# Attention probabilities kept as float32 and multiplied with the values as float32 products, two heads side by side

## The chip, the cores and the metric

The kernel runs on one core of one Trainium2 chip. The metric is the device time of one execution in microseconds (us), the median of several runs; less is better. Besides, one execution was recorded by the hardware profiler. Its engines are named as in the profile: PE is TensorE's matmul, PEld its weight load, DVE VectorE, ACT ScalarE, POOL GpSimd, SP SyncE, which issues the DMAs.

## The reference

A two-layer encoder on 1024 tokens of width 1024 in float32. The first layer mixes tokens by grouped-query attention, the second by a pooling mixer; each layer then cross-attends into 256 memory tokens and applies a gated MLP. The change touches the attention of the first layer alone, 16 query heads of width 64 that share 4 key and value heads:

```python
def axial_gqa_attention(h, w_qkv, q_gain, k_gain, w_o):
    ...
    def attend_block(q_blk):
        scores = jnp.einsum('bkgqd,bksd->bkgqs', q_blk, kt).astype(jnp.float32)
        p = jax.nn.softmax(scores, axis=-1).astype(vt.dtype)
        return jnp.einsum('bkgqs,bksd->bkgqd', p, vt)

    o = lax.map(attend_block, qb)
    o = o.transpose(1, 0, 4, 2, 3, 5).reshape(b, s, N_HEADS * HEAD_DIM)
    return o @ w_o
```

The softmax is over all 1024 keys (no mask).

## The kernel before

Nearly all products are done in a reduced float32 type (`float32r`, fp32r in the profile). To keep precision an operand is split in two such numbers, a high part (a cast) and a low part (what the cast left out), and the products of the parts are added. One tile pool of 20 slots of 128 x 2048 (`R`) holds the operands; `scr` is a ring of six 128 x 1024 float32 buffers.

The queries, keys and values come from a stage whose order a planner works out (engines, due times, a greedy schedule). It ends with the scores and softmax of the first three units (0 to 2). The values lie in two slots `V`, for each key block of 128 and each of the 4 value heads 128 columns: 64 of the high part, 64 of the low part.

Then comes the loop of the attention, whose order is written out by hand: each engine runs its instructions in the order of the program. A unit is 128 queries of one head; `units` lists (j, hh, i): j of 4 pairs of query blocks, hh of 16 heads, i of the two blocks of a pair: 128 units, numbered u. PSUM holds two score buffers of two banks each (`pA`) and four single banks (`pB`). The parts:

- `scores(u)`, L789: four products of 512 columns into one `pA`.
- `peak(u)`, L1189, on DVE: the negated row maximum. `softmax(u)`: exp with its sum on ACT (L1195), the sum's inverse on POOL as a power (L1197), the scaling on POOL (L1198). The probabilities are in a `scr` buffer, queries on the partitions.
- `turned(u)`, L1209: eight 128 x 128 transposes into two banks; ACT casts each bank into the high part (L1211). `lows(u)`, L1216: DVE subtracts that from the bank for the low part. `PT` holds two sets of a high and a low tile, one set for the two units of a head.
- `values(u)`, for odd u: both units of the head, so 256 columns. For each of 8 key blocks two products (L1231 with the high, L1232 with the low probabilities), with the 128 columns of values, high and low, loaded: the bank's upper and lower half have to be summed in the end. ACT copies one half into `osum` (L1237).
- `add(u)`: DVE adds the other half (L1243); at each second head POOL splits the sum of two heads into high and low part (L1246, L1247) in the slots `OT`, the operand of the output projection.

A turn of the loop treats two units: scores(u), peak(u), turned and lows of u-3 and u-2, softmax(u), scores(u+1), then `values(u - 3)`, peak(u+1), `add(u - 3)`, softmax(u+1). The last turns are written out one by one, with the values of the last heads between the transposes. After the loop the output projection follows (L756 to L758), and the rest of the kernel.

Of the kernel before, what the change touches and what calls it, by code (L numbers as in the profile page):

```python
# [23 lines left out]
HD = 64  # L24
NH = 16
NKV = 4
# [604 lines left out]
class Kernel:  # L631
# [140 lines left out]
    def attention(self):  # L772
        nc, R, a, tc = self.nc, self.R, self.a, self.tc
# [3 lines left out]
        V = [R.get() for _ in range(2)]  # L777
        units = [(j, hh, i) for j in range(NT // 2) for hh in range(NH) for i in range(2)]
        Q, prs, OT, sums = {}, {}, [], {}

        def score(u):
            j, hh, i = units[u]
            kv = hh // 4
            c0 = (j % 2 + 2 * i) * P
            q = R.v(Q[kv, j // 2], 4)[:, hh % 4, c0:c0 + P]
            s = self.psA()
            for kh in range(2):
                for part in range(2):
                    nc.tensor.matmul(s[:, kh * 512:(kh + 1) * 512], q,  # L789
                                     R.v(K[part][kh], 4)[:, kv],  # L790
                                     start=part == 0, stop=part == 1)
            return s

        with tc.tile_pool(name="qk", bufs=1, reuse_waits="tile") as qk, self.psum("psq", 1, 6) as self.ps:
# [3 lines left out]
            tabs, at, where = {"Q": tab}, {}, {}  # L798
# [22 lines left out]
            g = {"Q": self.cst.tile([P, HD], F32, name="gq"), "K": self.cst.tile([P, HD], F32, name="gk")}  # L821
# [351 lines left out]

        self.ps = self.ctx.enter_context(self.psum("ps", 2, 4))
        with tc.tile_pool(name="at", bufs=1, reuse_waits="tile") as at:
            PT = [[at.tile([P, 2048], F32R, name=f"PT{i}{j}") for j in range(2)] for i in range(2)]
            def parts(u):
                return (x.rearrange("p (a b) -> p a b", a=8) for x in PT[u // 2 % 2])

            S, nm, T = {}, {}, {}  # L1180

            def scores(u):
                if u not in prs:
                    S[u] = score(u)

            def peak(u):
                if u in S:
                    nm[u] = self.stat(1, "nm")
                    nc.vector.tensor_reduce(nm[u], S[u], axis=AX.X, op=OP.max, negate=True)  # L1189

            def softmax(u):
                if u in S:
                    pr = prs[u] = self.scr()
                    rs = self.stat(1, "sum")
                    nc.scalar.activation(pr, S.pop(u), AF.Exp, bias=nm.pop(u), accum_out=rs)  # L1195
                    ri = self.stat(1, "inv")
                    nc.gpsimd.tensor_tensor(out=ri, in0=rs, in1=self.minus, op=OP.pow)  # L1197
                    nc.gpsimd.tensor_scalar(pr, pr, ri, 1.0, op0=OP.mult, op1=OP.mult)  # L1198

            def pieces(u, g):  # L1200
                c = slice(u % 2 * P, (u % 2 + 1) * P)
                return (x[:, 4 * g:4 * g + 4, c] for x in parts(u))

            def turn(u, g):
                if u in prs:
                    p = T[u, g] = self.psB().rearrange("p (a b) -> p a b", a=4)
                    for k in range(4):
                        b = 4 * g + k
                        nc.tensor.transpose(p[:, k, :], prs[u][:, b * P:(b + 1) * P], self.ident)  # L1209
                    hi, _ = pieces(u, g)  # L1210
                    nc.scalar.copy(hi, p)  # L1211

            def low(u, g):
                if (u, g) in T:
                    hi, lo = pieces(u, g)
                    nc.vector.tensor_tensor(out=lo, in0=T.pop((u, g)), in1=hi.bitcast(F32), op=OP.subtract)  # L1216
                    if g:
                        del prs[u]

            def values(u, blocks=range(NT)):  # L1220
                if u > 0:
                    j, hh, i = units[u]
                    if blocks[0] == 0:
                        O[u] = self.psB()[:, :256]
                        if hh == 0:
                            OT.append([R.get(), R.get()])
                    ph, pl = parts(u)
                    o = O[u]
                    for kt in blocks:
                        v = R.tiles[V[kt // 4]].rearrange("p (k h c) -> p k h c", k=4, h=4)[:, kt % 4, hh // 4, :]  # L1230
                        nc.tensor.matmul(o, v, ph[:, kt], start=kt == 0, stop=False)  # L1231
                        nc.tensor.matmul(o, v, pl[:, kt], start=False, stop=kt == NT - 1)  # L1232
                    if blocks[-1] < NT - 1:
                        return
                    if hh % 2 == 0:
                        sums[0] = at.tile([P, 256], F32, name="osum", bufs=2)
                    nc.scalar.copy(sums[0][(hh % 2) * HD:(hh % 2 + 1) * HD], o[HD:])  # L1237

            def add(u):
                if u in O:  # L1240
                    j, hh, i = units[u]
                    oo = sums[0][(hh % 2) * HD:(hh % 2 + 1) * HD]
                    nc.vector.tensor_tensor(out=oo, in0=O.pop(u)[:HD], in1=oo, op=OP.add)  # L1243
                    if hh % 2:
                        hi, lo = (R.v(x, 8)[:, hh // 2] for x in OT[j])
                        nc.gpsimd.tensor_scalar(hi, sums[0], 1.0, 1.0, op0=OP.mult, op1=OP.mult)  # L1246
                        nc.gpsimd.tensor_tensor(out=lo, in0=sums[0], in1=hi.bitcast(F32), op=OP.subtract)  # L1247
                    if hh % 4 == 3 and j % 2:
                        R.put(Q[hh // 4, j // 2])

            O = {}
            with tc.manual_schedule():
                def turned(u):
                    for g in range(2):
                        turn(u, g)

                def lows(u):
                    for g in range(2):
                        low(u, g)

                def shared(u):

                    scores(u)
                    peak(u)
                    turned(u - 3)
                    turned(u - 2)
                    lows(u - 3)
                    lows(u - 2)
                    softmax(u)
                    scores(u + 1)  # L1270

                last = len(units) - 1
                for u in range(0, last - 1, 2):
                    shared(u)
                    values(u - 3)
                    peak(u + 1)
                    add(u - 3)
                    softmax(u + 1)
                shared(last - 1)
                peak(last)  # L1280
                turned(last - 2)
                lows(last - 2)
                softmax(last)
                values(last - 4)
                add(last - 4)
                turned(last - 1)
                lows(last - 1)
                values(last - 2, range(NT // 2))
                turned(last)
                lows(last)  # L1290
                values(last - 2, range(NT // 2, NT))
                add(last - 2)
                values(last)
                add(last)
            R.put(*V, *K[0], *K[1])
        return OT

# [8 lines left out]
    def cross(self, i, X, steps=None, mixer=None, over={}):  # L1306
# [168 lines left out]
        def plan_turn(plan, t):  # L1475
# [8 lines left out]
            def part(g, j):  # L1484
                if t % 2 not in PT:
                    PT[t % 2] = [R.get_pair() for _ in range(4)]
                pairs = PT[t % 2][2 * g:2 * g + 2]
                src = sm["ps", t][g].rearrange("p (a b) -> p a b", a=4)
                same = all(one[0] == other[0] for one, other in pairs[:j + 1])
                for ks in [slice(0, 4)] if same else [slice(0, 2), slice(2, 4)]:  # L1490
                    hi, lo = (R.blocks(z, ks, slice(t // 2 * P, (t // 2 + 1) * P)) for z in pairs)
                    self.low(hi, lo, src[:, ks]) if j else self.high(hi, src[:, ks])
            plan.add("turn", 8, emit, both(t), sorted(set(banks)), [("A", banks[0])] if t % 2 else [("B", k) for k in banks])
            for g in range(2):
                k = ("PT", t, g)
                plan.add("copy", 512, partial(part, g, 0), [banks[g]], [k], (), banks[g:g + 1], room=(("PT", t % 2), 8))
# [779 lines left out]
```

## Time and profile before

| | |
|---|---|
| median of 2 runs | 2498.97 us (2498.05 to 2499.89) |
| span of the profiled execution | 2493.0 us |
| the attention loop in it | about 178 to 528 us |
| matmuls of the loop's values (L1231, L1232) | 2 x 512, in 64 groups of 16 |
| scores (L789), transposes (L1209) | 512, 1024 |

The page gives busy time by engine, the chain of work that ended last and the groups of instructions; the trace can be asked for windows of time, for groups in a window and for the order of instructions (timeline). In a timeline a row is: start in us, duration in us, engine, line, operation, output and inputs, partitions x elements; a row with x4 merges four like instructions. In a group the count is followed by the total busy time in us and the mean duration in ns, then by the idle time before and what ended it. For a matmul, 128*128 128x512 stands for the loaded operand (rows*columns) and the one streamed through.

### The profile page before, as it was taken

The numbers are of one execution on the slowest core, as the hardware profiler recorded it, in microseconds if no ns is written. First come the engines' busy times: TensorE is split into PE (matmuls) and PEld (weight loads), VectorE is DVE, ScalarE is ACT, GpSimd is POOL, SyncE is SP. The second block draws the span as 40 slices with busy tenths as digits, with TensorE's granted clock in tenths as the row PEclk, the third lists the DMA queues.
The fourth block names the chain that finished last, engine by engine and source line by source line (L and its number), as shares of the span: only waits on it lengthen the run. The fifth ranks groups of instructions, "written<-read, shape, count | busy, mean of one in ns | idle before, by whom it ended". The sixth has DMA issues, their size and how long they took to land.

```text
span 2493.0 us, 37178 instructions
## 1 busy us (share of the span) xinstructions
PE 2474.6 (99%) x13510; PEld 2138.3 (86%) x13510; DVE 1991.6 (80%) x2839; ACT 1351.0 (54%) x2326; POOL 462.1 (19%) x658
## 2 busy tenths in 40 slices
PE   9999999999999999999999999999999999999998
PEld 9999999988899888888888888889888888888887
DVE  7879999974986389888889676997469888888875
ACT  6558888862655255455555334655345545554542
POOL 5767777731011000000000003102010000000001
PEclk9999999999999999999999999999999999999999
DMA  5300000042585124343258553388123324337852
GB/s 170 100 4 1 2 1 1 2 165 69 202 311 181 62 70 127 89 123 106 85 178 290 196 176 112 128 299 300 65 72 114 110 85 127 106 93 257 276 193 98
DMA packets 310124, 320.73 MB, mean 129 GB/s; under 512 B 13229, under 2 KB 244765, under 8 KB 309941
## 3 DMA queue, kind: packets, MB, share of 16 engines
q1 hardware_dynamic: 309941, 318.35, 38.8%
q8 instruction: 107, 1.75, 0.3%
q14 instruction: 76, 0.62, 0.1%
HBM read 230.91 MB, written 82.58 MB: 126 GB/s over the span
## 4 chain that ended last, share of the span: by engine, by line
PE 93%; issue 2%; DVE 2%; POOL 1%; ACT 1%; DMA 1%; SPq 0%; POOLq 0%; ACTq 0%; DVEq 0%
PE pB L756 22%; PE pB L758 22%; PE pB L757 22%; PE pA L789 5%; PE pB L1209 4%; PE pA L758 3%; PE pA L756 3%; PE pA L757 3%; PE pB L1231 2%; PE pB L1232 2%; PE pB L325 1%; DVE R L672 1%; PE pB L1072 1%; PE pA L2164 0%; DMA scr<-X 0%
## 5 line engine op out<-in xcount | busy, mean ns | idle before, releaser
L756 PE MATMUL pB<-R,R 128*128 128x512 f32 (+1 forms) x2732 | 1014.8, 371 | 1.8 <-ACT R L669 0.9
L758 PE MATMUL pB<-R,R 128*128 128x512 f32 (+1 forms) x2728 | 1007.6, 369 | 1.7 <-DVE R L672 1.6
L757 PE MATMUL pB<-R,R 128*128 128x512 f32 (+1 forms) x2732 | 1008.8, 369 | 0.2 <-DVE R L672 0.2
L756 PEld LDWEIGHTS pB<-R,R 128*128 128x128 f32 x2732 | 514.7, 188 | 90.9 <-ACT R L669 2.1
L758 PEld LDWEIGHTS pB<-R,R 128*128 128x128 f32 x2728 | 513.9, 188 | 89.5 <-DVE R L672 3.5
L757 PEld LDWEIGHTS pB<-R,R 128*128 128x128 f32 x2732 | 514.9, 188 | 87.1 <-DVE R L672 1.2
L669 ACT ACTIVATE R<-scr 128x512 fp32r<-128x512 f32 (+2 forms) x340 | 256.8, 782 | 214.9 <-DMA scr<-Gs 59.8
L729 POOL TENSOR_SCALAR ms<-ss 128x1 f32<-128x1 f32 (+2 forms) x97 | 32.1, 331 | 1651.7 <-ACT R L737 1279.9
L672 DVE TENSOR_TENSOR R<-X,R 128x512 fp32r<-128x512 f32 x374 | 252.0, 685 | 67.8 <-ACT R L669 67.1
L669 ACT ACTIVATE R<-X 128x512 fp32r<-128x512 f32 x374 | 231.8, 630 | 132.9 <-PE pB L757 64.0
L672 DVE TENSOR_TENSOR R<-scr,R 128x512 fp32r<-128x512 f32 (+2 forms) x328 | 275.0, 867 | 26.6 <-ACT R L669 26.2
L439 ACT COPY scr<-pB 128x512 f32<-128x512 f32 x156 | 91.3, 585 | 180.6 <-PE pB L758 173.3
L1852 DVE TENSOR_TENSOR X<-pB,X 128x512 f32<-128x512 f32 (+1 forms) x145 | 99.2, 685 | 80.4 <-PE pB L758 79.6
L1216 DVE TENSOR_TENSOR PT<-pB,PT 128x512 fp32r<-128x512 f32 x256 | 159.1, 683 | 4.2 <-ACT PT L1211 2.9
L1189 DVE TENSOR_REDUCE nm<-pA 128x1 f32<-128x1024 f32 x125 | 152.2, 1218 | 4.3
L756 PE MATMUL pA<-R,R 128*128 128x512 f32 (+1 forms) x420 | 150.6, 359 | 0.0
L758 PE MATMUL pA<-R,R 128*128 128x512 f32 (+1 forms) x420 | 150.2, 358 | 0.0
L757 PE MATMUL pA<-R,R 128*128 128x512 f32 (+1 forms) x420 | 149.9, 357 | 0.0
L1195 ACT ACTIVATE scr<-pA,nm 128x1024 f32<-128x1024 f32 x125 | 142.4, 1139 | 5.6 <-DVE nm L1189 3.5
L789 PE MATMUL pA<-R,R 128*128 128x512 f32 x512 | 144.7, 404 | 0.3 <-ACT scr L1195 0.3
L1198 POOL TENSOR_SCALAR scr<-scr,inv 128x1024 f32<-128x1024 f32 x125 | 141.2, 1129 | 12.3
L1211 ACT CAST PT<-pB 128x512 fp32r<-128x512 f32 x256 | 131.0, 600 | 1.2 <-PE pB L1209 1.2
(184 smaller groups left out, 3582.5 us busy)
## 6 DMA issues: line engine op xcount, KB each, us to landing
X<-in_ffn_w_up SPq DMA_DIRECT2D x82, 512.0 KB
Gs<-X SPq DMA_DIRECT2D x105, 256.0 KB
scr<-in_ffn_w_down SPq DMA_DIRECT2D x45, 512.0 KB
scr<-Gs SPq DMA_DIRECT2D x35, 512.0 KB
scr<-in_xattn_w_kv SPq DMA_DIRECT2D x32, 512.0 KB
scr<-Gs SPq DMA_DIRECT2D x42, 384.0 KB
scr<-in_attn_w_qkv SPq DMA_DIRECT2D x22, 512.0 KB
Wt<-scr SPq DMA_DIRECT2D x44, 256.0 KB
```

The lines of the kernel that those rows point to most:

```text
L669: self.nc.scalar.activation(hi, src, AF.Copy)
L672: self.nc.vector.tensor_tensor(out=lo, in0=src, in1=hi.bitcast(F32), op=OP.subtract)
L756: mm(out, ah, bh, start=start, stop=False)
L757: mm(out, ah, bl, start=False, stop=False)
L758: mm(out, al, bh, start=False, stop=stop)
L789: nc.tensor.matmul(s[:, kh * 512:(kh + 1) * 512], q, R.v(K[part][kh], 4)[:, kv], start=part == 0, stop=part == 1)
L1189: nc.vector.tensor_reduce(nm[u], S[u], axis=AX.X, op=OP.max, negate=True)
L1195: nc.scalar.activation(pr, S.pop(u), AF.Exp, bias=nm.pop(u), accum_out=rs)
L1198: nc.gpsimd.tensor_scalar(pr, pr, ri, 1.0, op0=OP.mult, op1=OP.mult)
L1209: nc.tensor.transpose(p[:, k, :], prs[u][:, b * P:(b + 1) * P], self.ident)
L1211: nc.scalar.copy(hi, p)
L1216: nc.vector.tensor_tensor(out=lo, in0=T.pop((u, g)), in1=hi.bitcast(F32), op=OP.subtract)
```

## The change

The probabilities stay float32. After the transposes one bank of a unit is copied by ACT and the other by DVE; there is no split and no subtraction. `PT` is now three float32 tiles, each for the two units of a head, so it takes three tiles in place of four.

The values are summed back to float32 before the loop: POOL adds high and low part into `V32`, in two instructions.

The products with the values are float32 products. They come for two heads at once, at every fourth unit (u % 4 = 3), so in every second turn: for each key block one product for the first head into partitions 0 to 63 of a bank and one for the second head into partitions 64 to 127, each with 64 columns of values loaded and 256 columns streamed. The bank then holds the result of both heads, and `hi_lo` (ACT casts, DVE subtracts) splits it straight into `OT`. `osum` goes. The slots `OT` are taken with the first group of values of a pair of query blocks.

The order in a turn is otherwise the same, and `add` still comes between `peak(u + 1)` and `softmax(u + 1)`. The last turns aren't written out any more: the loop runs two turns longer, in which nothing but transposes and values is left.

```diff
-            PT = [[at.tile([P, 2048], F32R, name=f"PT{i}{j}") for j in range(2)] for i in range(2)]
...
+            PT = [at.tile([P, 2048], F32, name=f"PT{i}").rearrange("p (a b) -> p a b", a=NT) for i in range(3)]
+            V32 = at.tile([P, 2048], F32, name="V32").rearrange("p (k h c) -> p k h c", k=NT, h=NKV)
...
-            def turn(u, g):
-                if u in prs:
-                    p = T[u, g] = self.psB().rearrange("p (a b) -> p a b", a=4)
+            def turned(u):
+
+                if u not in prs:
+                    return
+                for g in range(2):
+                    p = self.psB().rearrange("p (a b) -> p a b", a=4)
                     for k in range(4):
                         b = 4 * g + k
                         nc.tensor.transpose(p[:, k, :], prs[u][:, b * P:(b + 1) * P], self.ident)
-                    hi, _ = pieces(u, g)
-                    nc.scalar.copy(hi, p)
-
-            def low(u, g):
-                if (u, g) in T:
-                    hi, lo = pieces(u, g)
-                    nc.vector.tensor_tensor(out=lo, in0=T.pop((u, g)), in1=hi.bitcast(F32), op=OP.subtract)
...
+                    out = PT[u // 2 % 3][:, 4 * g:4 * g + 4, u % 2 * P:(u % 2 + 1) * P]
+                    (nc.vector.tensor_copy if g else nc.scalar.copy)(out, p)
+                del prs[u]
+
+            def values(u):
+
+                j, hh, _ = units[u]
+                o = O[u] = self.psB()[:, :256]
+                if hh == 1:
+                    OT.append([R.get(), R.get()])
+                for kt in range(NT):
+                    for x in range(2):
+                        nc.tensor.matmul(o[x * HD:(x + 1) * HD], V32[:, kt, hh // 4], PT[(u // 4 * 2 + x) % 3][:, kt],
+                                         start=kt == 0, stop=kt == NT - 1)
 
             def add(u):
...
+                j, hh, _ = units[u]
+                self.hi_lo(*(R.v(x, 8)[:, hh // 2] for x in OT[j]), O.pop(u))
+                if hh % 4 == 3 and j % 2:
+                    R.put(Q[hh // 4, j // 2])
...
+                for s in range(2):
+                    v4 = R.tiles[V[s]].bitcast(F32).rearrange("p (k h c) -> p k h c", k=4, h=NKV)
+                    nc.gpsimd.tensor_tensor(out=V32[:, 4 * s:4 * s + 4], in0=v4[..., :HD], in1=v4[..., HD:], op=OP.add)
+                for u in range(0, last + 4, 2):
+                    there = u <= last
+                    if there:
+                        scores(u)
+                        peak(u)
                     turned(u - 3)
                     turned(u - 2)
...
+                    if there:
+                        softmax(u)
+                        scores(u + 1)
+                    v = u - 3
+                    if v >= 3 and v % 4 == 3:
+                        values(v)
+                    if there:
+                        peak(u + 1)
+                    if v >= 3 and v % 4 == 3:
+                        add(v)
+                    if there:
+                        softmax(u + 1)
```

More of the change, by code (lines that the diff above doesn't have):

```diff
@@ L1239, in add @@
-            def add(u):
[L1240 to L1249, printed above, removed]
+                    out = PT[u // 2 % 3][:, 4 * g:4 * g + 4, u % 2 * P:(u % 2 + 1) * P]
@@ L1261, in shared @@
-                def shared(u):
-                    scores(u)
-                    peak(u)
+                last = len(units) - 1
+                for s in range(2):
[6 more added lines that the diff above has]
+                        peak(u)
@@ L1265, in shared @@
                     turned(u - 3)
                     turned(u - 2)
[L1267 to L1294, printed above, removed]
+                    if there:
+                        softmax(u)
+                        scores(u + 1)
```

33 lines of the change are left out of this document (1 added, 32 removed).

## The prediction

> **What bounds the kernel now.** I read the page from the top, then the attention loop (200 to 515 us) by its windows, its groups and one turn of its timeline. The page's first two parts, and one stretch of the windows view (us, then busy time and count of PE, PEld, DVE, ACT, POOL, then granted clock, DMA share, GB/s):
>
> ```profile
> span 2493.0 us, 37178 instructions
> PE 2474.6 (99%) x13510; PEld 2138.3 (86%) x13510; DVE 1991.6 (80%) x2839; ACT 1351.0 (54%) x2326; POOL 462.1 (19%) x658
> 200.00:250.00 50.00, 50.00 (x368) 46.34 (x365) 48.01 (x65) 42.58 (x85) 35.91 (x48) 1.00 0.00 1
> ```
>
> TensorE is never idle in the loop, at a granted clock of 1.00, and nothing is fetched. VectorE stands at 96%, ScalarE at 85%: close behind, but behind. A turn of the loop treats one head (two units of 128 queries). In order of time, on PE, ACT and DVE:
>
> ```profile
> 301.59 1.09 PE L789 MATMUL pA<-R,R 128*128 128x512 f32 x4
> 302.52 1.91 PE L1209 MATMUL pB<-ident,scr 128*128 128x128 f32 x16
> 304.18 1.17 PE L789 MATMUL pA<-R,R 128*128 128x512 f32 x4
> 305.19 0.28 PE L1231 MATMUL pB<-PT,R 128*128 128x256 f32 x1
> ...
> 306.96 0.28 PE L1232 MATMUL pB<-PT,R 128*128 128x256 f32 x1
> 307.07 0.40 PE L789 MATMUL pA<-R,R 128*128 128x512 f32 x1
> 302.19 1.12 ACT L1195 ACTIVATE scr<-pA,nm 128x1024 f32<-128x1024 f32 x1
> 303.29 2.04 ACT L1211 CAST PT<-pB 128x512 fp32r<-128x512 f32 x4
> 305.19 1.16 ACT L1195 ACTIVATE scr<-pA,nm 128x1024 f32<-128x1024 f32 x1
> 306.20 0.24 ACT L1195 ACTIVATION_READ_ACCUMULATOR scr<-pA,nm 128x1 f32 x1
> 302.72 1.23 DVE L1189 TENSOR_REDUCE nm<-pA 128x1 f32<-128x1024 f32 x1
> 303.98 2.48 DVE L1216 TENSOR_TENSOR PT<-pB,PT 128x512 fp32r<-128x512 f32 x4
> ```
>
> The turn repeats after 307.07 - 301.59 = 5.48 us: scores 0.93, sixteen transposes 1.66, scores 1.01, values 1.88. Matmuls overlap their own drains, so cost is read from start to start: a 512-column product takes 0.93 / 4 = 0.2325 us, a 256-column one of the values 1.88 / 16 = 0.1175 us, although their rows last 0.4 and 0.28. One wait is covered only narrowly: the exp of the unit whose scores began at 301.59 ends at 306.35, 4.76 us later, and the scores at 307.07 need its bank pair. There are 0.72 us to spare.
>
> **The change, part by part.** *The products.* Per pair of heads, 32 products of 256 columns in fp32r (3.76 us) go and 16 float32 products of 256 columns come. What one of those costs, no row says: the only float32 products, of the pooling stage, are narrower. Their rows (the code asks for 80, the profile counts 144 + 16), with the weight loads of the two forms, and two fp32r groups for the slope:
>
> ```profile
> L2164 PE MATMUL pA<-scr 128*128 128x112 f32 x144 | 17.3, 275 | 1.0 <-PE pA L2164 0.6 <-POOL scr L2150 0.4
> L2164 PE MATMUL pA<-scr 24*128 24x16 f32 x16 | 2.0, 259 | 0.0
> 1524.16 1.98 PEld L2164 LDWEIGHTS pA<-scr 128*128 128x128 f32 x16
> 1524.38 1.93 PE L2164 MATMUL pA<-scr 128*128 128x112 f32 x16
> 1565.11 1.86 PEld L2164 LDWEIGHTS pA<-scr 24*128 24x128 f32 x16 [0.17 <-POOL rs L731]
> 1565.11 1.95 PE L2164 MATMUL pA<-scr 24*128 24x16 f32 x16
> L756 PE MATMUL pB<-R,R 128*128 128x512 f32 x2214 | 865.4, 391 | 0.9 <-DVE R L672 0.7
> L756 PE MATMUL pB<-R,R 128*128 128x256 f32 x518 | 149.3, 288 | 0.9 <-ACT R L669 0.9
> ```
>
> So each float32 product runs as two records, each with its own weight load. Sixteen records take the same 0.11 us each with 112 columns ((1.93 - 0.275) / 15) as with 16 columns ((1.95 - 0.259) / 15): the loads of 128 columns set that pace, and the stream itself is hidden. Its bounds for 256 columns are 0.1175 us (no slower than fp32r) and 256 / 112 x 0.11 = 0.25 us. I take 0.2325, two streams per record, for this reason: the last 112-column record ends 0.17 us after its last load (1526.31 against 1526.14), the 16-column one 0.09 us (1567.06 against 1566.97). That is 0.08 us for 96 columns, 0.83 ns each, against (391 - 288) / 256 = 0.40 ns in fp32r. It isn't clean, since the rows differ too (24 against 128), but the upper bound is also the nearer one.
>
> A pair of heads then has 8 key blocks x 2 heads x 2 records = 32 records of 0.2325 us: 7.44 us one after the other, 3.72 us if the two column halves stream beside each other. All products in the rows above load 128 columns; none shows two halves at work, so this is the open question. I take beside each other: the two heads load other columns and write other partitions, and what the rows show of TensorE (the next product begins 0.1175 us after one that lasts 0.28, and loads run beside streams) is an engine that waits for the columns a stream holds, not for its end. To the 3.72 I add, for the middle, half of what two exposed loads per key block would cost (64 columns, half of 0.11 us: 8 x 2 x 0.055 = 0.9 us): 4.2 us, between 3.7 and 4.6.
>
> The Trainium skill, "TensorEngine Tiling (Array Packing)", Key Properties, says that tiles run loads and matmuls in parallel, but that a change of the tiling mode drains the engine. No run here shows either yet; by the second, two drains of about 0.16 us in each of 32 groups would put some 10 us on top, 2546 us. The skill's "TensorE: Matmul & The Clock Gate", Measured speedup vs the span model, gives 2.38 for three column tiles; an estimate from it is 7.44 / (2 x 2.38 / 3) = 4.7 us for a pair, and the sum would be 2551 us.
>
> *The copies.* Per unit, two casts on ACT (2.04 us for four) and two subtractions on DVE (2.48 for four) become one copy on each: per turn ACT loses about 1.0 us and DVE 1.24. Neither engine carried the turn, so this gains nothing by itself. The sum of the two halves on ACT, DVE and POOL becomes a cast and a subtraction per pair of heads, off the path except as below.
>
> *The new order.* Values now come in every second turn only. A turn without them has 0.93 + 1.66 + 1.01 = 3.60 us of TensorE work, less than the 4.76 us after which the exp frees the scores' banks. With two copies less on ACT that becomes 3.8 at the least; but the second copy still waits for the second unit's transposes, so I take 4.15: a stall of 0.55 us (bounds 0.1 and 1.1). In the next turn the transposes of that unit wait for the exp's read, the power and the scaling on POOL; that adds 0.1. The add is queued on ACT ahead of the next exp, so that exp waits for the whole group of values; it then ends some 1.7 us into the next turn, ahead of that turn's copies, and costs nothing more. Two turns: 7.20 + 0.65 + 4.2 = 12.05 us against 10.96, +1.09 us, 31 times: +33.8 us.
>
> *The ends.* The float32 values are built by two POOL sums of 1024 columns before the loop's first softmax. The rows, and those of the old end of the loop:
>
> ```profile
> L343 POOL TENSOR_TENSOR X<-X,X 128x512 f32<-128x512 f32 x6 | 7.8, 1293 | 31.2 <-DVE X L343 31.2
> 183.50 0.56 POOL L1197 TENSOR_TENSOR inv<-sum,minus 128x1 f32<-128x1 f32 x1 [5.23 <-ACT scr L1195]
> 304.64 1.13 POOL L1198 TENSOR_SCALAR scr<-scr,inv 128x1024 f32<-128x1024 f32 x1
> 521.48 0.28 PE L1232 MATMUL pB<-PT,R 128*128 128x256 f32 x1
> 528.19 0.39 PE L756 MATMUL pB<-R,R 128*128 128x512 f32 x1
> L669 ACT ACTIVATE R<-pB 128x256 fp32r<-128x256 f32 x36 | 14.0, 389 | 34.6 <-PE pB L758 34.6
> ```
>
> Two sums of twice 1.29 us are 5.2 us, and POOL idles 5.23 us there: nothing, or a microsecond if it doesn't fit. At the end, old TensorE took 528.19 - 521.48 - 0.12 = 6.6 us from the values of unit 123 to the next stage. Now the last exp waits for those values (0.17) and their cast (0.39); then exp and its read 1.25, power 0.55, scaling 1.13, transposes 0.9, copy 0.6: 5.0 us, with hand-overs 5.2; then the last values, 4.2: 9.4, or +2.8. The sum: +33.8 + 2.8 = +36.6 us, a profiled span of 2530. The profiled span is 6 us under the median of the runs, 2498.97, and what lies around it stays: 2499 + 37 = **2536 us**.
>
> **The rivals.** *One half after the other.* The slower side. Both halves are fed by one queue that starts products in order, and no row shows two streams at once; if a second stream waits for the first, whatever columns it uses, values cost 7.44 us: 7.85 + 7.44 - 10.96 = +4.33 us a pair, 134 us, and with an end 6 us longer 2639 us. It decides from values of about 4.6 us a pair on, where 2% is passed. For it: every start in the rows follows the former by a full stream. Chance 0.36.
>
> *One stream per record.* If a record streams its columns once, as the lower bound allows, values cost 3.76 us one after the other (7.85 + 3.76, +0.65 us a pair: 2521 us) or 1.88 beside each other (-1.23 us a pair: 2462 us). Against it is the 0.83 ns a column. Chance 0.06, half for each.
>
> *VectorE set the turn.* At 96% it nearly did; then its relief would show as a shorter turn. But TensorE has no idle in the loop, so the gain is nil, and I count no chance for it apart from the forecast.
>
> **How the numbers follow.** The forecast's chance is 0.58. Its own range: with a stall of 0.1 in place of 0.65 and values of 3.72, 11.0 us for two turns, 2503; with 1.1 + 0.1 and 4.6, 13.0 us, 2566. The range of 8 in 10 runs from 2503 to 2650: it takes in the middle and three quarters of the first rival, whose own ends lie some 20 us to either side, and leaves out about 0.09 above and 0.05 below. Two per cent (about what a measurement of this kernel can tell from no change) is 50 us: under 2449 lies no case worked out here, 0.02 is left for one; over 2549 lie the first rival, 0.36, and a bit over a quarter of the forecast, 0.16: 0.52. Within is the rest, 0.46.
>
> **What would show it.** In the changed profile: the start-to-start time in the group of values, 32 records in 3.7 to 4.6 us, or in 7.4 (the whole question); the time between groups of values, 12 us or 15; a gap on TensorE before the second scores after a group, released by the exp, of about half a microsecond; ACT's cast of the output ahead of a late exp; DVE in the loop down to about 65% (four peaks of 1.23, four copies of 0.62, 0.4 for the output, in 12.05 us); POOL's two sums between 178 and 184 us. The prediction is wrong if the records start closer than 0.11 us apart (another cost of float32), if a turn without values takes 3.6 us (no stall), or if the difference lies outside the loop.

## The result and the profile after

The changed kernel took 2526.29 us (median of 2523.58 and 2529.0) against 2498.97 us before: 1.0109 of the time before, interval 1.008 to 1.0138. Four more runs of it (the first experiment) gave 2524.65 us, 1.0104 [1.0089, 1.0119]. It is slower by about 27 us, within the 2% that counts as no change.

The first lines of the page of the changed kernel, and the same stretch of the windows view as before (us; busy time and count of PE, PEld, DVE, ACT, POOL; granted clock, DMA share, GB/s):

```profile
span 2527.2 us, 36303 instructions
PE 2489.8 (99%) x13510; PEld 2089.1 (83%) x13510; DVE 1905.0 (75%) x2679; ACT 1279.8 (51%) x2166; POOL 429.9 (17%) x596
200.00:250.00 50.00, 48.34 (x347) 36.30 (x347) 33.93 (x40) 31.10 (x58) 29.08 (x36) 1.00 0.01 1
```

The count of matmuls is the same (13510), since 32 fp32r products per pair of heads became 16 float32 products of two records each. DVE fell from 96% to 68% of the stretch, ACT from 85% to 62%. But PE, which had no idle time, now has some: 48.34 of 50 us.

Where it sits is read from the timeline of PE, over one pair of heads (start, duration, engine, line, operation, shapes, idle time before and its releaser):

```profile
299.63 1.20 PE L789 MATMUL pA<-R,R 128*128 128x512 f32 x4
300.67 1.91 PE L1206 MATMUL pB<-ident,scr 128*128 128x128 f32 x16
302.33 1.18 PE L789 MATMUL pA<-R,R 128*128 128x512 f32 x4
303.92 1.19 PE L789 MATMUL pA<-R,R 128*128 128x512 f32 x4 [0.41 <-ACT scr L1193]
304.95 1.91 PE L1206 MATMUL pB<-ident,scr 128*128 128x128 f32 x16
306.62 1.17 PE L789 MATMUL pA<-R,R 128*128 128x512 f32 x4
307.72 3.67 PE L1219 MATMUL pB<-PT,V 128*64 128x256 f32 x32
311.32 0.50 PE L789 MATMUL pA<-R,R 128*128 128x512 f32 x1
```

The pair takes 311.32 - 299.63 = 11.69 us, against 2 x 5.48 = 10.96 before. From start to start, beside the two old turns:

| step | after | before | difference |
|---|---|---|---|
| scores (299.63) | 1.04 | 0.93 | +0.11 |
| transposes | 1.66 | 1.66 | 0 |
| scores (302.33), to the next scores | 1.59 | 1.01 | +0.58 |
| scores (303.92), after the gap | 1.03 | 0.93 | +0.10 |
| transposes | 1.67 | 1.66 | +0.01 |
| scores (306.62), to the values | 1.10 | 1.01 | +0.09 |
| values | 3.60 | 2 x 1.88 | -0.16 |
| sum | 11.69 | 10.96 | +0.73 |

The largest entry is the turn without values. Its second scores start at 302.33 and would be done at 302.33 + 0.93 = 303.26; the next ones start at 303.92, 0.66 us later. ACT tells why (same columns):

```profile
300.03 1.11 ACT L1193 ACTIVATE scr<-pA,nm 128x1024 f32<-128x1024 f32 x1
301.30 0.58 ACT L1208 COPY PT<-pB 128x512 f32<-128x512 f32 x1
302.17 0.59 ACT L1208 COPY PT<-pB 128x512 f32<-128x512 f32 x1 [0.29 <-PE pB L1206]
302.65 1.12 ACT L1193 ACTIVATE scr<-pA,nm 128x1024 f32<-128x1024 f32 x1
304.86 1.12 ACT L1193 ACTIVATE scr<-pA,nm 128x1024 f32<-128x1024 f32 x1 [0.99 <-DVE nm L1187]
```

The exp that starts at 302.65 reads the scores of 299.63. It stands behind two copies, the second of which waits for the last transposes of the turn, and it ends at 303.77; the scores at 303.92 write the banks that it read. The exp before it (300.03), which was late because its engine had waited for the whole group of values, ends at 301.14 and holds up nobody.

The small entries (+0.11, +0.09) lie where the array goes from full columns to halves and back. PEld, the weight loads, stops there for the reason "issue", which means that it waited for nothing the profile shows:

```profile
307.72 3.22 PEld L1219 LDWEIGHTS pB<-PT,V 128*64 128x64 f32 x32 [0.36 <-issue]
311.32 0.30 PEld L789 LDWEIGHTS pA<-R,R 128*128 128x128 f32 x2 [0.39 <-issue]
```

Within the group of values the records start in pairs: the second of a pair 6 to 7 ns after the first, and the next pair 0.216 us later (0.267 after the first pair). The rows don't name the head of a record. That a pair is one record of each head is read from the experiment e2 below, where the second head has to wait at the start of the group: there two records run alone first (305.467 and 305.734), then 14 pairs follow, then again two alone (309.022 and 309.238). So the halves stream side by side, and 16 pairs take 3.45 us.

The end of the loop, PE:

```profile
541.60 3.67 PE L1219 MATMUL pB<-PT,V 128*64 128x256 f32 x32
548.70 1.09 PE L1206 MATMUL pB<-ident,scr 128*128 128x128 f32 x8 [1.53 <-POOL scr L1196]
549.72 4.03 PE L1219 MATMUL pB<-PT,V 128*64 128x256 f32 x32
553.68 0.50 PE L756 MATMUL pB<-R,R 128*128 128x512 f32 x1
```

From the end of the values of unit 123 (541.60 + 3.60 = 545.20) to the next stage it takes 8.5 us, before 6.6: +1.9. Together: 31 x 0.73 + 1.9 = 24.5 us. Read straight from the traces, from the loop's first transpose to the first product of the next stage, it is a little less: 528.19 - 178.47 = 349.7 us before and 553.68 - 180.34 = 373.3 us after, +23.6 us (there are 30 full pairs between the first and the last regular group, at +0.71 on average, and the first turns cost 0.4). Beside that stand 25.7 us between the medians of the changed kernel's four further runs and of the runs of before beside them (2524.65 and 2498.92). The two profiled executions differ by more, 2527.2 - 2493.0 = 34.2 us; that is taken up with the last of the experiments.

### The profile page after: what moved, and what is told of

It reads as the page before. It is cut to its first block, busy times and chain, and to the rows that moved or that the text cites. A ratio compares the mean times of both kernels' runs of the same rounds, so it can differ in the third digit from the quotient of the medians.

```text
span 2527.2 us, 36303 instructions
## 1 busy us (share of the span) xinstructions
PE 2489.8 (99%) x13510; PEld 2089.1 (83%) x13510; DVE 1905.0 (75%) x2679; ACT 1279.8 (51%) x2166; POOL 429.9 (17%) x596
## 4 chain that ended last, share of the span: by engine, by line
PE 88%; issue 3%; DVE 3%; DMA 2%; ACT 2%; POOL 1%; SPq 0%; POOLq 0%; DVEq 0%; ACTq 0%
PE pB L756 21%; PE pB L758 21%; PE pB L757 21%; PE pB L1219 4%; PE pA L789 4%; PE pB L1206 4%; PE pA L758 3%; PE pA L756 3%; PE pA L757 3%; ACT scr L1193 1%; DVE R L672 1%; PE pB L325 1%; DMA scr<-in_ffn_w_down 1%; PE pB L1072 1%; DMA scr<-X 0%
## 5 line engine op out<-in xcount | busy, mean ns | idle before, releaser
L672 DVE TENSOR_TENSOR R<-scr,R 128x512 fp32r<-128x512 f32 (+2 forms) x328 | 275.5, 868 | 26.4 <-ACT R L669 25.7
L789 PE MATMUL pA<-R,R 128*128 128x512 f32 x512 | 151.3, 417 | 13.3 <-ACT scr L1193 13.3
L789 PEld LDWEIGHTS pA<-R,R 128*128 128x128 f32 x512 | 86.4, 188 | 49.7 <-ACT scr L1193 26.9
L1206 PEld LDWEIGHTS pB<-ident,scr 128*128 128x128 f32 x1024 | 114.9, 140 | 12.5 <-POOL scr L1196 1.8
```

Of the source, the lines that this page charges most:

```text
L672: self.nc.vector.tensor_tensor(out=lo, in0=src, in1=hi.bitcast(F32), op=OP.subtract)
L789: nc.tensor.matmul(s[:, kh * 512:(kh + 1) * 512], q, R.v(K[part][kh], 4)[:, kv], start=part == 0, stop=part == 1)
```

## The experiments

All times are per program, with the ratio to the kernel before run beside it on the same chip and its 95% interval; "a pair" is the time from one group of values to the next (two turns).

| run | us | ratio [interval] | a pair |
|---|---|---|---|
| e1_again | 2524.65 | 1.0104 [1.0089, 1.0119] | 11.71 |
| e2_exp_first | 2525.11 | 1.0107 [1.0092, 1.0122] | 11.69 |
| e3_add_late | 2521.84 | 1.0096 [1.0079, 1.0113] | 11.69 |
| e4_both | 2524.64 | 1.0104 [1.0089, 1.0119] | 11.69 |
| e5_exp_first_short_turns | 2511.65 | 1.0049 [1.0035, 1.0063] | 11.24 |
| e6_short_turns_add_late | 2510.04 | 1.0040 [1.0028, 1.0053] | 11.24 |
| e7_halves_apart | 2608.01 | 1.0433 [1.0414, 1.0452] | 14.35 |
| e8_full_columns | 2620.55 | 1.0483 [1.0464, 1.0502] | 14.80 |
| e9_bf16 | 2445.04 | 0.9788 [0.9770, 0.9805] | 9.09 |
| e11_low_parts_in_halves | 2496.69 | 0.9995 [0.9986, 1.0004] | 2 x 5.43 |
| e12_bf16_short_turns | 2460.84 | 0.9854 [0.9838, 0.9871] | 9.66 |

**The changed kernel again**, to have a base with an interval:

> The changed kernel once more, as the measure for the runs beside it. In its profile a pair of heads takes 11.69 us in the loop (10.96 before), which is +0.73 x 31 = +23 us; the theory puts the whole difference there and expects a ratio of 1.009 to 1.011 and stages outside the loop as before. The rival, that part of the cost lies behind the loop (the first profile was 9 us longer there), expects some 9 us outside the loop again.

11.71 us a pair and 2524.65 us: the account above stands in a second execution, whose loop takes 373.7 us. Behind the loop this execution is again 6 to 7 us longer than the first profile of before, as the rival had it; the last of the experiments shows what that is worth.

**The order on ACT.** Two places in the order could cost the gap: the exp behind the copies, and the exp behind the `add`. Each was moved alone, then both.

```diff
                         scores(u)
                         peak(u)
+                    if there:
+                        softmax(u)
                     turned(u - 3)
                     turned(u - 2)
                     if there:
-                        softmax(u)
                         scores(u + 1)
```

> ACT runs the first unit's exp ahead of the two copies in place of behind them; nothing else changes. Theory (the stall of the turn without values is the exp waiting behind the second copy): the exp follows its peak, 3.6 us after its scores began, the gap of 0.66 us before the scores of the next turn goes, up to 0.2 us of it comes back as a wait for the scaled probabilities: 11.2 us a pair of heads, -15 us, about 2511 us. Rival (the loss is the switching of TensorE to half the columns and back, or the wait only moves to the copies): no change, 11.6 to 11.7 us a pair, 2526 us.

```diff
                         peak(u + 1)
+                        softmax(u + 1)
                     if v >= 3 and v % 4 == 3:
                         add(v)
-                    if there:
-                        softmax(u + 1)
```

> The split of the values' result is queued on ACT and DVE behind the exp of the turn's second unit, so that this exp no longer waits for the end of the values. Theory (that exp ends long before it is needed, and the gap is set by the first unit's exp behind its copies): no change, within 3 us of the changed kernel. Rival (the late exp pushes ACT's copies and the next exp back and so makes the gap): up to 0.66 us a pair less, -20 us, 2506 us.

> Both edits: the first exp ahead of the copies, and the split of the result behind the second exp. Theory: as the exp ahead alone, 11.2 us a pair, about 2511 us, since the late exp cost nothing; what is left over the 10.96 us of before is the switching (about 0.4 us a pair) less the 0.3 us that the float32 products save. Rival (both waits count): 11.0 us or less, 2500 us, no difference from before.

With the exp first, most of the gap before the scores is gone, yet the pair is as long as it was. PE of that run, then ACT, and two rows of its waits between 200 and 515 us (total, times, longest):

```profile
300.56 2.31 PE L789 MATMUL pA<-R,R 128*128 128x512 f32 x8
302.70 1.91 PE L1206 MATMUL pB<-ident,scr 128*128 128x128 f32 x16
304.37 1.17 PE L789 MATMUL pA<-R,R 128*128 128x512 f32 x4
305.47 4.15 PE L1219 MATMUL pB<-PT,V 128*64 128x256 f32 x32
309.55 1.19 PE L789 MATMUL pA<-R,R 128*128 128x512 f32 x4
```

```profile
304.22 1.12 ACT L1193 ACTIVATE scr<-pA,nm 128x1024 f32<-128x1024 f32 x1
305.32 1.06 ACT L1208 COPY PT<-pB 128x512 f32<-128x512 f32 x2
```

```profile
PEld pB L1219 <- DVE PT L1208: 9.7, 27, 0.4
PEld pB L1219 <- ACT PT L1208: 7.8, 27, 0.3
```

The eight scores now merge into one row and take 302.70 - 300.56 = 2.14 us in place of 304.95 - 302.33 = 2.62, so 0.48 us less; free of waits they would take 8 x 0.2325 = 1.86, so a part of the gap is left. But in the turn with values both copies stand behind the exp of 304.22 and run from 305.32 to 306.38, when the values have already begun. The group of values takes 309.55 - 305.47 = 4.08 us in place of 3.60, so 0.48 us more: the second head's records start only at 305.950, behind the first of the two copies. Of the two rows of waits the second is this one. The first is nothing new: the changed kernel has the same 0.36 us each time as "issue" (9.8 us, 27 times), on the way into the halves. The wait moved from the exp to the copies, as the rival of that run had it, and the 2511 us of its theory were missed.

Moving the `add` alone changed no pair in the loop: 11.69 us. It only brought the last two groups of values closer together, 6.37 us apart in place of 8.12. So the exp that waits for the group of values costs nothing in the loop. Both edits together missed the 2511 us expected of them, for the reason shown by the first.

**The exp first only where no values follow.** If both waits are real, the order has to differ between the two turns:

```diff
+                    if there and u % 4 == 0:
+                        softmax(u)
                     turned(u - 3)
                     turned(u - 2)
                     if there:
-                        softmax(u)
+                        if u % 4:
+                            softmax(u)
                         scores(u + 1)
```

> ACT runs the first unit's exp ahead of the two copies only in the turns without values; in the turns with values the copies stay first. Theory (exp first took the gap of 0.66 us away, down to about 0.2, but in the turn with values it put two exps ahead of the copies that the values wait for, and their group grew from 3.67 to 4.15 us): both are right now, 11.2 us a pair of heads, -14 us against the changed kernel, about 2511 us. Rival (something else holds the pair at 11.69 us, so that each wait removed comes back elsewhere): 11.69 us again, 2525 us.

> The same with the split of the values' result queued behind the second exp. Theory: the same 11.2 us a pair, and the end of the loop 1.7 us shorter, as the late split alone made it: 2509 us. Rival: as the run beside it.

PE of the first of the two, one pair, and the weight load that still waits for the exp:

```profile
304.45 1.22 PE L789 MATMUL pA<-R,R 128*128 128x512 f32 x4
305.50 1.91 PE L1206 MATMUL pB<-ident,scr 128*128 128x128 f32 x16
307.17 2.31 PE L789 MATMUL pA<-R,R 128*128 128x512 f32 x8
309.32 1.91 PE L1206 MATMUL pB<-ident,scr 128*128 128x128 f32 x16
310.98 1.17 PE L789 MATMUL pA<-R,R 128*128 128x512 f32 x4
312.09 3.67 PE L1219 MATMUL pB<-PT,V 128*64 128x256 f32 x32
```

```profile
308.28 0.76 PEld L789 LDWEIGHTS pA<-R,R 128*128 128x128 f32 x4 [0.38 <-ACT scr L1193]
```

11.24 us a pair and 2511.65 us, where 11.2 and 2511 were expected: about half of the loss (13 of 25.7 us) is this one place in the order, and it is shown by undoing it alone. The sequence from 307.17 to 309.32 takes 2.15 us where 8 x 0.2325 = 1.86 were free of waits, so a gap of 0.2 to 0.3 us is left. The second edit adds what it gave before at the end (last groups 6.37 us apart). 2510.04 us is the best that was reached with float32 probabilities, and its interval still lies above 1.

**The halves one after the other, and not at all.** The prediction's open question was whether two column halves stream at once. In the first of these two kernels the halves stay, but all products of one head come before those of the other. In the second the full columns are used, high and low values at 64 columns each, one head after the other; this kernel leaves out the sum of the two partial results of a head.

```diff
-                for kt in range(NT):
-                    for x in range(2):
+                for x in range(2):
+                    for kt in range(NT):
```

> The products of the first head all come ahead of those of the second, so that neighbours in the queue use the same half of the columns; instructions and results are the same. Theory (two halves stream beside each other, a record holding its half for 0.216 us): 32 records one after another, 6.9 us in place of 3.5, 15.1 us a pair of heads, +107 us and 3 at the end, 2635 us. Rival (the halves never run beside each other and a record streams its columns once): no change, 2525 us.

```diff
-                o = O[u] = self.psB()[:, :256]
+                o = O[u] = self.psB()
...
-                for kt in range(NT):
-                    for x in range(2):
-                        nc.tensor.matmul(o[x * HD:(x + 1) * HD], V32[:, kt, hh // 4], PT[(u // 4 * 2 + x) % 3][:, kt],
+                for x in range(2):
+                    for kt in range(NT):
+                        v = R.tiles[V[kt // 4]].bitcast(F32).rearrange("p (k h c) -> p k h c", k=4, h=NKV)[:, kt % 4, hh // 4]
+                        nc.tensor.matmul(o[:, x * 256:(x + 1) * 256], v, PT[(u // 4 * 2 + x) % 3][:, kt],
...
-                self.hi_lo(*(R.v(x, 8)[:, hh // 2] for x in OT[j]), O.pop(u))
+                self.hi_lo(*(R.v(x, 8)[:, hh // 2] for x in OT[j]), O.pop(u)[:, :256])
```

> Float32 products with all 128 columns loaded (high and low values as float32 numbers), one head after the other into the two halves of a bank; the two partial sums of a head are not added, which leaves that out of the result. No half columns, no switching. Theory: 32 records of 0.227 us, 7.3 us, less some 0.4 us of switching: 14.9 us a pair of heads, +100 us against the changed kernel, about 2627 us, a little under the run with the halves apart. Rival (switching costs nothing): the same time as with the halves apart plus 0.3 us a pair, 2645 us.

The groups of values on PE, of the first and of the second:

```profile
305.22 6.31 PE L1219 MATMUL pB<-PT,V 128*64 128x256 f32 x32
```

```profile
306.93 7.07 PE L1220 MATMUL pB<-PT,R 128*128 128x256 f32 x32
```

With full columns a record starts every (7.07 - 0.38) / 31 = 0.2158 us (0.38 us is the duration of the last one): just the pace at which a pair of half-column records starts in the changed kernel. So a float32 record costs the time of two streams of 256 columns (a pair of bfloat16 records, below, starts every 0.109 us), 128-column loads lie wholly behind it, and the halves give the full factor of two. The rest of the pair, without the streams, is 14.80 - 32 x 0.2158 = 7.89 us with full columns and 11.69 - 16 x 0.2158 = 8.24 us with halves, both with the same gap of 0.41 us before the scores. The difference, 0.35 us, is what the change to halves and back costs a pair; in the table above it is the 0.11, the 0.09 and the 0.15 us by which the group of values is longer than its streams. Over 31 pairs this is 11 us. It also closes the account of the best float32 order above: 0.35 for the change and 0.2 to 0.3 for the rest of the gap, less the 3.76 - 3.45 = 0.31 that the products save, is close to the 11.24 - 10.96 = 0.28 us that were left. The Trainium skill, "TensorEngine Tiling (Array Packing)", Key Properties, says that a change of the tiling mode (here from full columns to halves) drains the engine. The trace agrees in so far as each change costs time, 0.35 us for the way in and back; that this time is a drain no row says.

The halves one after the other lost 2.66 us a pair against the changed kernel (14.35 - 11.69), so it is the order of issue that lets them stream together. They lost less than the full 16 x 0.2158 = 3.45 us, and less than the 15.1 us a pair and 2635 us expected; the last section comes back to that.

**What the products alone are worth.** The same kernel with bfloat16 probabilities and values, which keep fewer digits:

```diff
-            PT = [at.tile([P, 2048], F32, name=f"PT{i}").rearrange("p (a b) -> p a b", a=NT) for i in range(3)]
-            V32 = at.tile([P, 2048], F32, name="V32").rearrange("p (k h c) -> p k h c", k=NT, h=NKV)
+            PT = [at.tile([P, 2048], mybir.dt.bfloat16, name=f"PT{i}").rearrange("p (a b) -> p a b", a=NT) for i in range(3)]
+            V32 = at.tile([P, 2048], mybir.dt.bfloat16, name="V32").rearrange("p (k h c) -> p k h c", k=NT, h=NKV)
```

> The changed kernel with probabilities and values of the value products rounded to bfloat16, which takes precision away; order and shapes are the same. It takes the price of float32 out and leaves the turns and the switching. Theory (a float32 product is two records of two streams, a bfloat16 one a single stream): 8 pairs of 0.11 us, 0.9 us in place of 3.5; gap and switching stay, so 9.1 us a pair of heads, -80 us, 2445 us. Rival (ACT or DVE is close behind TensorE and takes over): 9.9 us a pair or more, 2470 us or more.

```profile
304.14 1.19 PE L789 MATMUL pA<-R,R 128*128 128x512 f32 x4 [0.42 <-ACT scr L1193]
...
307.94 1.06 PE L1219 MATMUL pB<-PT,V 128*64 128x256 bf16 x16
308.94 1.19 PE L789 MATMUL pA<-R,R 128*128 128x512 f32 x4
```

9.09 us and 2445.04 us, as expected: the values fell from 3.60 to 1.00 us, and all of that came off the pair, with the gap where it was. TensorE's streams carry the loop, and neither ACT nor DVE took over. This version beats both kernels, by 2.1% against the kernel before (interval 2.0% to 2.3%), at a lower precision of the probabilities and values.

Then the order of the two short-turn runs was put into it:

> Probabilities and values of the value products in bfloat16, as in the run before, with the first exp ahead of the copies in the turns without values and the split of the result behind the second exp. Theory (the gap of 0.66 us does not depend on what the values cost, and goes as it did with float32): 8.6 to 8.7 us a pair of heads, 1.7 us less at the end, -14 us against bfloat16 alone, 2431 us. Rival (with values of 1 us in place of 3.6 the copies and the exp of the next turn no longer fit beside them, and the wait stays): 9.1 us a pair, 2443 us.

It missed, theory and rival: 9.66 us a pair, worse than without. DVE, ACT and PE there, in order of time:

```profile
307.51 0.39 ACT L677 ACTIVATE R<-pB 128x256 fp32r<-128x256 f32 x1
307.93 0.42 DVE L678 TENSOR_TENSOR R<-pB,R 128x256 fp32r<-128x256 f32 x1 [1.62 <-ACT R L677]
308.27 1.22 DVE L1187 TENSOR_REDUCE nm<-pA 128x1 f32<-128x1024 f32 x1
309.58 1.11 ACT L1193 ACTIVATE scr<-pA,nm 128x1024 f32<-128x1024 f32 x1 [1.68 <-DVE nm L1187]
310.84 1.20 PE L789 MATMUL pA<-R,R 128*128 128x512 f32 x4 [0.82 <-ACT scr L1193]
```

With the split of the output after the exp, ACT's cast (307.51) comes late; DVE's subtraction waits 1.62 us for it, and the next peak is queued behind the subtraction. The exp then waits for the peak and the scores for the exp. With float32 values the same order cost nothing (the run at 2510.04 us); that the longer group of values, 3.60 us against 1.00, is what covers it there is an inference. Two edits went in at once, and the exp first alone, in bfloat16, wasn't tried.

**Another use of the halves**, in the kernel before: there the low probabilities became bfloat16 and were multiplied with a bfloat16 copy of the high values, even key blocks in one half and odd ones in the other. The products of low with low are left out.

```diff
...
-                        nc.tensor.matmul(o, v, ph[:, kt], start=kt == 0, stop=False)
-                        nc.tensor.matmul(o, v, pl[:, kt], start=False, stop=kt == NT - 1)
+                        nc.tensor.matmul(o, v, ph[:, kt], start=kt == 0, stop=False, skip_group_check=True)
+                    for kt in blocks:
+                        x = kt % 2
+                        nc.tensor.matmul(o[x * HD:(x + 1) * HD], V16[:, kt, hh // 4], pl[:, kt], start=False, stop=kt >= NT - 2,
+                                         skip_group_check=True)
...
```

> The kernel before, with only the products of the low probabilities moved to column halves: low probabilities and a copy of the high values in bfloat16, neighbouring key blocks side by side into the two halves that are summed anyway; the product of low with low is left out. Theory (two halves stream beside each other, a change to halves and back costs 0.35 us): a turn has eight products of 0.1175 us, four pairs of 0.11 and one change, 1.73 in place of 1.88 us: 5.33 us a turn if DVE, busy 5.25 of 5.48 us, keeps up; -8 us, 2490 us, faster than both. Rival (DVE takes over, or the change costs more beside fp32r): 5.48 us or more, 2499 us or slower.

PE over the values of one turn, then a row of its waits between 200 and 500 us:

```profile
304.22 1.09 PE L1233 MATMUL pB<-PT,R 128*128 128x256 f32 x8
305.25 0.63 PE L1236 MATMUL pB<-PT,V 128*64 128x256 bf16 x8
305.94 1.19 PE L789 MATMUL pA<-R,R 128*128 128x512 f32 x4
```

```profile
PEld pA L789 <- ACT scr L1197: 17.6, 55, 0.3
```

No difference: 0.9995 [0.9986, 1.0004]. The values fell from 1.88 to 305.94 - 304.22 = 1.72 us, as expected, but the turn only from 5.48 to 5.43, and 2490 us were missed. The next scores now wait for the exp in 55 turns, up to 0.3 us; 0.2 of that is the way back to full columns, which the bfloat16 kernel shows without such a wait. The prediction's "0.72 us to spare" of the old turn was for one exp; the peaks and exps behind it leave less. The exp in its turn waits for its peak on DVE, which is busy for 299.56 of the 315 us between 200 and 515 us. So the rival of this run, that DVE takes over, isn't ruled out.

**The kernel before, profiled once more**, for the rest of the 34.2 us between the two profiled executions:

> The kernel before, profiled once more, for what lies outside the attention loop. Its first profile had 1965 us from the loop's last values to the end, the changed kernel and its variants 1970 to 1974. If that is chance of the one execution, 1966 to 1970 here and a span of 2495 to 2498; if the change costs time behind the loop, 1965 again.

Its span was 2497.8 us, 4.8 more than in the first profile, with 2499.55 us for the run. Its loop takes 349.7 us, as in the first profile, while the changed kernel's loop takes 373.3 and 373.7 us in its two: so the loop accounts for 23.6 to 24.0 us. What is left of the 34.2 us lies on both sides of it. The loop begins at 180.34 us here and in the first profile of the changed kernel, at 178.47 in the first of before and at 179.12 in the repeat of the changed kernel, so that isn't the change. From the last product with the values to the end of the span it took 1967.8 us here, in the first profile 1965, and between 1968.7 and 1974.8 in the twelve executions with a changed loop, of which the changed kernel's own two gave 1973.8 and 1971.7. So at least 3 us of the difference behind the loop come and go between executions of one kernel. Whether some of the other 4 to 6 us belongs to the change stays open; by the interval of the repeat, 0.89% to 1.19% of 2499 us, the whole change costs 22 to 30 us.

## Why the prediction was right

Forecast were 2536 us, within 2%; it was 2526.29. The chances leaned the other way by a little: 0.52 for more than 2% slower, nearly all of it through the first rival, and 0.46 for what came.

- **The halves stream side by side.** Right: pairs of records 6 ns apart, 0.216 us per pair. The rival, one half after the other, would have been 2639 us; the two kernels in which the records were made to follow one another came out at 2608 and 2621.
- **A float32 record streams its columns twice.** Right, and the rival of one stream per record is out: 0.2158 us against 0.1175 for a 256-column fp32r product. The 0.2325 taken was 8% too long; with it the streams came to 3.72 us in place of 3.45. So the 32 records took 3.60 us, below the 3.7 to 4.6 of the forecast, and start 0.106 us apart on average (3.30 us from the first start to the last), just under the 0.11 that the prediction named as a sign of being wrong. That sign was set too near: the cost of a float32 record is the forecast one of two streams, and it is the length of a stream that was taken too long.
- **Exposed loads.** Wrong, a term that did not exist: half of two loads per key block were put at nearly 0.5 us. Loads of 64 and of 128 columns both lie behind the streams. What was there instead is the change to halves and back, 0.35 us a pair, which the sum did not hold; the sentence on the Trainium skill had estimated it at 10 us for the loop, and 11 were measured. Values and change together are 3.45 + 0.35 = 3.80 us, forecast 4.2. That this came so near is in part luck: the term that wasn't there stood in for the one that was missing. The Trainium skill's other figure in the prediction, 2.38 for three column tiles ("TensorE: Matmul & The Clock Gate", Measured speedup vs the span model), would by the prediction's estimate have made it 4.7 us; with two halves the trace shows a factor of 2.
- **The stall of the turn without values.** Right in place and cause: the second copy holds back the exp, and the exp the scores. 0.66 us measured, 0.55 forecast. Undoing it gave 0.45 us a pair and 13 us in all.
- **The wait for the scaling in the next turn**, 0.1 us. Not there: the transposes at 304.95 follow their scores in 1.03 us, and the 0.10 more than before lies within the scores, whose second record starts 0.33 us after the first in place of 0.2325 (303.919 and 304.251). It is a cost of the start after the gap, which no term of the sum held; by its size it took the place of the wait.
- **The late exp costs nothing more.** Right: with the `add` behind it no pair was shorter.
- **The copies gain nothing by themselves.** Right: DVE went from 96% to 68% (forecast about 65%) and ACT from 85% to 62%, while the loop grew longer.
- **POOL's two sums are hidden.** Right. They run from 180.10 to 184.83, 2.4 us each; ACT's exp and its read end at 184.84, and the inverse that waits for both follows at 184.92:

```profile
184.65 0.19 ACT L1193 ACTIVATION_READ_ACCUMULATOR scr<-pA,nm 128x1 f32 x1
180.10 4.73 POOL L1233 TENSOR_TENSOR V<-R 128x1024 f32<-128x1024 f32 x2
184.92 0.56 POOL L1195 TENSOR_TENSOR inv<-sum,minus 128x1 f32<-128x1 f32 x1
```

- **The end of the loop.** +2.8 us forecast, +1.9 measured.

The forecast's pair was 12.05 us, 0.36 too long: 0.40 for values and change together, less 0.04 for the turn without values, where 0.58 + 0.10 + 0.01 = 0.69 us more than the old turn stand against 0.65. Over 31 pairs that is 11 us, with the end 12: 36.6 - 12 = 24.5, the sum of the rows above (23.6 straight from the traces). The prediction also set the profiled span 6 us under the median of the runs. The span is about 1.8 us shorter than the time of the same run (2527.2 and 2529.0; 2497.8 and 2499.55); the other 4 us were that one execution.

## What to carry to other kernels

In this loop, where TensorE never idled, relief of two engines at 96% and 85% bought nothing, and the cost was what TensorE streams plus the waits that the new order opened: products 0.31 us a pair cheaper were outweighed by one late exp (0.66) and by changes of the column tiling (0.35). When work is gathered into every second turn, look at the turn left without it: what it used to cover now shows, and its order on the in-order engines may have to differ from that of the other turn, because moving the wait in all turns only handed it to what was queued behind (11.69 us a pair again). Before packing small groups into column halves, set the change to halves and back, 0.35 us a group here, against the streams saved.

## What the hardware showed that was not expected

- With all products of one head ahead of the other's, the two halves still ran together for a while. In the trace of that kernel the starts follow two series of 0.216 us each: one begins at 305.216 and has its 16th record at 308.504; the other begins at 307.863, when three of the first series have not started. The rows don't say which head a record belongs to, so the two series are read from the pace and from the longer first record of each (0.43 us against 0.38). It fits the 6.31 - 0.38 = 5.93 us of the group, where 31 steps of 0.2158 would be 6.69.
- The pace of 0.2158 us for two streams of 256 columns is shorter than the 0.2325 us of one fp32r product of 512 columns from the same kind of rows, though as many columns are streamed if a float32 record streams its columns twice.
- The 128-column loads, to which the prediction put the pace of 0.11 us of the narrow float32 products of the pooling stage, are hidden completely behind records of 0.2158 us.
